# Matrix-memory gate rows: computed per tile inside the mLSTM chain, or per block of four tiles in a chain of their own

## The chip, the cores and the metric

The kernel runs on one core of a Trainium2 chip. The metric is the device time of one execution in microseconds (us), the median over several runs. The engines of the core are TensorE (PE, with the weight load PEld beside it), VectorE (DVE), ScalarE (ACT), GpSimd (POOL) and SyncE (SP), which issues the DMAs. SBUF is the on-chip memory of 128 partitions, PSUM the accumulation memory that TensorE writes. L1103 means line 1103 of the kernel.

## The reference

One layer of a hybrid encoder over 2048 prompt tokens and 8 x 16 sample tokens, width 1024, all in float32. An input projection gives queries, keys, values and gates of a matrix memory (mLSTM, 4 heads of 128) and of a sliding-window attention (8 query heads, 2 key/value heads of 64). Their outputs are joined, projected, added to the input and normalised; then come a ConvFFN (up to 2 x 2816 columns, causal convolution of width 3, gate, down to 1024) and another normalisation. What the change touches is the stabiliser of the matrix memory:

```python
b = jnp.cumsum(lf, axis=-1)                     # log forget gates, per head
inter = b + m[..., None]                        # m: running maximum carried between chunks
dmat = jnp.where(causal, b[..., :, None] - b[..., None, :] + li[..., None, :], -jnp.inf)
mt = jnp.maximum(inter, jnp.max(dmat, axis=-1))
w_inter = jnp.exp(inter - mt)
s = jnp.einsum('bhld,bhsd->bhls', qc, kc) * jnp.exp(dmat - mt[..., None])
num = w_inter[..., None] * jnp.einsum('bhld,bhde->bhle', qc, C) + jnp.einsum('bhls,bhse->bhle', s, vc)
h = num / jnp.maximum(jnp.abs(den), jnp.exp(-mt))[..., None]
m_new = jnp.maximum(b_last + m, jnp.max(g, axis=-1))    # g = b_last - b + li
```

With a = li - b this needs, for each head and token l, the running maximum M(l) of m and of all a up to l; then mt = b + M, the first weight is exp(m - M(l)) and the second exp(a(s) - M(l)) for s <= l. After a tile, m becomes b(last) + M(last).

## The kernel before

The tokens are 17 tiles of 128: 16 of the prompt, and tile 16 with the sample tokens. Matmuls run in fp32r on operands that are split into a high and a low part (three products for one); the large projections save an eighth of the products with a scheme of seven products for eight. Weights come by DMA into four raw slots and are split into high and low halves by ScalarE (L220) and VectorE (L221), into a ring of eight halves, later ten.

By the trace the stages are: the input projection (PE lines L734 and L759) until about 650 us, in four blocks of tiles (`IBLOCKS`: tiles 0 to 3 with 16, then 4 to 7, 8 to 11, 12 to 15); the output projection (L225 to L227) until about 890, in the blocks `OBLOCKS`; the up-projections of the feed-forward (L1875) from 930 to 1880; its down-projections (L2079) to the end. The work per token tile, which is little and full of waits, is woven into the dense matmuls: `t_sample` (the sample tile, 179 to 290 us), `m_chain` (the matrix memory, prompt tiles 0 to 15, 292 to 876) and `a_chain` (the attention) are generators. Each `yield cost, latency, banks` says how much PE time the step just emitted costs, how long the next step's inputs need, and how many of five PSUM banks the next step wants; `weave` emits the next step of a chain when its due time has passed by its own estimate of time. So the order of PE's instructions is fixed by these estimates when the program is built (`manual_schedule`, PE only); the order on the other engines is made by a scheduler from the data dependences and priorities. SP issues all DMAs from one queue in order.

A prompt tile in the matrix memory goes so. `m_load` issues the loads of q, k, v and the output gate. `m_rows` transposes the log gates of the tile to rows (four heads on four partitions, 128 tokens: `pgr`, L1033 and L1034), scans them for b (L1103), subtracts (L1104), scans for M with the carry `mc` as its start value (L1105), splits M in high and low for a matmul (`hilo`), makes the row -b - M (`y_row`, L1044) and the new carry. In `m_tile`, `m_rep` puts -M(l) of each head on all 128 partitions with four matmuls against a selection matrix (`pm`, L1127); `m_cols` turns the rows a and -b - M, and the carry, into columns (`pcol`, L1051 and L1052, copied to SBUF at L1055); `m_masked` adds the causal mask (L1132), and ScalarE takes exp with the column as bias: `m_inter` (L1144), `m_exps` (L1138), `m_emt` (L1060). Scores, products with v and with the state C, the state's update, the normalisation `m_norm` (its maximum is L1180) and `m_out` follow. The output stage reads the mixed rows of a block with `x_pair` (its subtraction is L926, for some of them on GpSimd).

Of the kernel before, what the change touches and what calls it, by code (L numbers as in the profile page):

```python
# [18 lines left out]
DB = 8  # L19
DS = 16  # L20
NPT = SEQ // P
NT = NPT + 1
TOK = NT * P
MH = 4
# [9 lines left out]
NBANKS = 5  # L34
HOLDS = {"pm": 6500, "pgr": 4000, "pnum": 5000, "ppo": 6500}

# [3 lines left out]
IBLOCKS = [[0, 1, 2, 3, 16], [4, 5, 6, 7], [8, 9, 10, 11], [12, 13, 14, 15]]  # L40
# [116 lines left out]
class Chains:  # L157
# [47 lines left out]
class Prog:  # L205
# [96 lines left out]
    def setup(self):  # L302
        nc, a, cp, dp = self.nc, self.a, self.cp, self.dp
# [4 lines left out]
        nc.vector.memset(self.mhalf, -0.5)  # L308
        self.zqk = [dp.tile([8, P, P * len(b)], F32, name=f"zqk{i}") for i, b in enumerate(IBLOCKS)]
        self.zws = [[dp.tile([1 if g < KEPT else 2, P, 4, HT], F32, name=f"zws{g}_{i}") for i in range(4)] for g in range(NG)]  # L310
        self.zv = [dp.tile([P, 512], F32, name=f"zv{t}") for t in range(NT)]
# [648 lines left out]
    def t_setup(self):  # L960
        nc, a, tp = self.nc, self.a, self.tp
# [17 lines left out]

        raw = self.work("kw", [36, MH])  # L980
        nc.sync.dma_start(raw, a["sel"])
        self.sel = self.one("sel", [36, MH], F32R)
        nc.vector.tensor_copy(self.sel, raw)
        self.hl = [self.one(f"hl{i}", [36, P], F32R) for i in range(2)]
        self.ay = [self.one(f"ay{i}", [36, P]) for i in range(2)]
        for i in range(2):
            nc.vector.memset(self.ay[i], 0.0)
            nc.vector.tensor_copy(self.hl[i], self.ay[i])
# [4 lines left out]
        self.mc = self.one("mc0", [MH, 1])  # L993
        nc.vector.memset(self.mc, 0.0)

# [6 lines left out]
    def gate_logs(self, b):  # L1002

        nc, tp = self.nc, self.tp
        n = len(IBLOCKS[b])
        g = tp.tile([P, 5, 8], F32, name="g1", tag="g1", bufs=2)
        nc.vector.tensor_add(g[:, :n], self.gates[b][:, :n], self.gb.rearrange("p (o m) -> p o m", o=1).to_broadcast([P, n, 8]))
        x = g[:, :n, 0:4]
# [18 lines left out]
    def row(self, nm, dt=F32):  # L1027
        return self.work("r_" + nm, [MH, P], dt, 1 if nm == "b" else 2)

    def gate_rows(self, g, i):  # L1030

        ps = self.bank([MH, 2, P], "pgr")
        self.nc.tensor.transpose(ps[:, 0], g[:, i, 0:4], self.ident)  # L1033
        self.nc.tensor.transpose(ps[:, 1], g[:, i, 4:8], self.ident)  # L1034
        return ps[:, 0], ps[:, 1]

    def hilo(self, i, src):

        nc, dst = self.nc, self.hl[i]
        nc.vector.tensor_copy(dst[0:4], src)  # L1040
        nc.vector.tensor_sub(dst[32:36], src, dst[0:4].bitcast(F32))

    def y_row(self, i, b, M):
        self.nc.vector.scalar_tensor_tensor(self.ay[i][32:36], b, -1.0, M, op0=ALU.mult, op1=ALU.subtract)  # L1044

    def m_cols(self, i, mp=None):

        nc = self.nc
        ps = self.bank([P, 40], "pcol")
        if mp is not None:  # L1050
            nc.tensor.matmul(ps[:, 0:4], mp.to_broadcast([MH, P]), self.ident[:MH, :MH], start=True, stop=True)  # L1051
        nc.tensor.transpose(ps[:, 4:40], self.ay[i], self.ident[:36, :36])  # L1052
        c0 = 4 if mp is None else 0
        col = self.work("col", [P, 40], bufs=2)
        nc.vector.tensor_copy(col[:, c0:], ps[:, c0:])  # L1055
        return col

    def m_emt(self, col):
        emt = self.work("emt", [P, MH], bufs=2)
        self.nc.scalar.activation(emt, col[:, 36:40], AF.Exp)  # L1060
        return emt

# [9 lines left out]
    def m_chain(self):  # L1072
        nc = self.nc
        while not self.chains.done["s"]:
            yield 0, 500
        pend = None
        for t in range(NPT):
            b, ti = self.place(t)
            while self.i_done <= b:
                yield 0, 500  # L1080
            if pend is None:
                pend = self.m_load(t, b, ti), *self.m_rows(t, b, ti)
                yield 300, 7000, 2
            else:
                yield 0, 1000, 2
# [4 lines left out]
            if t + 1 < NPT and self.i_done > self.place(t + 1)[0]:  # L1090
                pend = self.m_load(t + 1, *self.place(t + 1)), *self.m_rows(t + 1, *self.place(t + 1))
            yield 300, 6800, 1
            self.m_out(t, hn[0])
            self.chains.done["m"] = t
        nc.sync.dma_start(self.a["m_p"], self.mc)
        nc.sync.dma_start(self.a["cn_p"], self.C)

    def m_rows(self, t, b, ti):
        V = self.nc.vector
        lf, li = self.gate_rows(self.logs_of(b), ti)  # L1100
        i = t % 2
        bc, a_, M = self.row("b"), self.ay[i][0:4], self.row("M")
        V.tensor_tensor_scan(bc, lf, self.seg[:, 0], 0.0, op0=ALU.add, op1=ALU.add)  # L1103
        V.tensor_sub(a_, li, bc)  # L1104
        V.tensor_tensor_scan(M, self.seg[:, 0], a_, self.mc, op0=ALU.add, op1=ALU.max)  # L1105
# [16 lines left out]

    def m_rep(self, i):

        pm = self.bank([P, MH, P], "pm")
        for h in range(MH):
            self.nc.tensor.matmul(pm[:, h], self.sel[:, h:h + 1].to_broadcast([36, P]), self.hl[i], start=True, stop=True)  # L1127
        return pm

    def m_masked(self, pm, mask):  # L1130
        dt = self.work("dt", [P, MH, P])
        self.nc.vector.tensor_tensor(dt, pm, mask.rearrange("p (o m) -> p o m", o=1).to_broadcast([P, MH, P]), op=ALU.add)  # L1132
        return dt

    def m_exps(self, dt, col):

        for h in range(MH):
            self.nc.scalar.activation(dt[:, h], dt[:, h], AF.Exp, bias=col[:, 4 + h:5 + h])  # L1138

    def m_inter(self, pm, col):  # L1140

        wi = self.work("wi", [P, MH, P])
        for h in range(MH):
            self.nc.scalar.activation(wi[:, h], pm[:, h], AF.Exp, bias=col[:, h:h + 1])  # L1144
        return wi
# [61 lines left out]

    def m_tile(self, t, load, i, mp):
        nc = self.nc
        V = nc.vector  # L1210
        qk, v1, og = load
        pm = self.m_rep(i)
        col = self.m_cols(i, mp)
        dt = self.m_masked(pm, self.mcau)
        yield 600, 2800
        emt = self.m_emt(col)
        wi = self.m_inter(pm, col)
        self.m_exps(dt, col)
        yield 0, 5000, 2
# [161 lines left out]
    def t_sample(self):  # L1381
        nc, a = self.nc, self.a
        V = nc.vector
        t = NPT
# [4 lines left out]
        b, ti = self.place(t)  # L1389
        lf, li = self.gate_rows(self.logs_of(b), ti)  # L1390
        bc, M = [self.row(n) for n in ("b", "M")]
        ar = self.work("sd", [MH, P], name="ar")
        a_ = self.ay[1][0:4]
        V.tensor_tensor_scan(bc, self.seg[:, 1], lf, 0.0, op0=ALU.mult, op1=ALU.add)
# [9 lines left out]
        b3 = lambda r: r.rearrange("p (b l) -> p b l", b=DB)  # L1404
        V.tensor_sub(b3(x), b3(M), self.m0.rearrange("p (b o) -> p b o", o=1).to_broadcast([MH, DB, DS]))
        self.hilo(0, x)
        self.hilo(1, M)
        self.y_row(1, bc, M)
# [7 lines left out]
        col = self.m_cols(1)  # L1416
        dt = self.m_masked(pm, mblk)
        emt = self.m_emt(col)
        self.m_exps(dt, col)
# [751 lines left out]
```

## Time and profile before

| | |
|---|---|
| runs | 2345.95, 2350.46, 2352.51 us; median 2350.46 |
| profiled execution | 2345.55 us, span 2343.8 us |
| PE busy | 2304.7 us, 98% of the span |
| VectorE busy | 1805.6 us, 77% |
| ScalarE busy | 1298.6 us, 55% |
| GpSimd busy | 244.7 us, 10% |
| DMA | 624.98 MB, mean 267 GB/s |

The span runs from the first to the last instruction of the profiled execution; its own time is a little longer. Busy times of different engines overlap. Matmuls overlap each other too, so the time that one takes from PE is read from the distance between starts, not from its duration. In rows of a tile's instructions the three numbers behind the count are the least, the median and the greatest duration in ns, followed by the stretch of the span in which they lie.

### The profile page before, as it was taken

The page shows a single profiled execution, that of the slowest core. Times are in us where ns is not written, and L with a number is a line of the kernel's source. Part 1 is how long each engine was busy: PE and PEld are TensorE (multiplying, and loading weights), DVE is VectorE, ACT ScalarE, POOL GpSimd, SP SyncE. Part 2 cuts the span into 40 slices and gives each one's busy share as a digit, 9 for nine tenths or more (in the row PEclk, how much of TensorE's full clock was granted, in tenths as well). Part 3 has the DMA queues.
Part 4 walks back from the last instruction along what each step waited for, and adds up shares of the span by engine and source line. Part 5 has one row for each costly group of instructions (what it writes and reads, how often), then busy time and mean ns, then how long its engine had stood idle before and what let it go on. Part 6 is the DMA issues. An engine that isn't in the chain of part 4 may idle for free.

```text
span 2343.8 us, 39880 instructions
## 1 busy us (share of the span) xinstructions
PE 2304.7 (98%) x14425; PEld 2116.7 (90%) x14425; DVE 1805.6 (77%) x3150; ACT 1298.6 (55%) x2465; POOL 244.7 (10%) x298
## 2 busy tenths in 40 slices
PE   8999999999999999999999999999999999999998
PEld 8989998999987777999999999999999978888887
DVE  8676586797688888987888777768766776796897
ACT  5353466676666665555556555545544544654653
POOL 0101101101112221300001000002000100000100
PEclk9999999999999999999999999999999999999999
DMA  8888889889877667787777889878988776756753
GB/s 277 285 306 287 290 280 319 283 280 340 296 256 246 215 206 268 269 323 275 279 270 252 309 314 320 303 272 264 316 289 261 241 278 212 237 193 222 238 184 108
DMA packets 297365, 624.98 MB, mean 267 GB/s; under 512 B 47052, under 2 KB 140240, under 8 KB 297168
## 3 DMA queue, kind: packets, MB, share of 16 engines
q1 hardware_dynamic: 296304, 619.29, 77.6%
q10 hardware_dynamic: 864, 3.15, 0.4%
q8 instruction: 114, 1.87, 0.3%
q14 instruction: 83, 0.68, 0.1%
HBM read 451.78 MB, written 170.56 MB: 266 GB/s over the span
## 4 chain that ended last, share of the span: by engine, by line
PE 72%; DVE 6%; DMA 2%; issue 2%; ACT 2%; POOL 0%; SPq 0%; DVEq 0%; ACTq 0%; POOLq 0%
PE fup L1875 18%; PE dps L1875 18%; PE dps L2079 6%; PE dps L734 6%; PE fup L2079 6%; PE fht L2079 5%; PE dps L225 2%; PE dps L227 2%; PE dps L226 2%; PE ppo L1370 1%; PE psc L1321 1%; PE ppt L1364 1%; PE dps L759 1%; DVE hl L221 1%; DVE w L221 1%
## 5 line engine op out<-in xcount | busy, mean ns | idle before, releaser
L1875 PE MATMUL dps<-hh,uw 128*128 128x384 f32 (+1 forms) x1848 | 480.6, 328 | 6.8 <-ACT u L1900 1.9
L1875 PE MATMUL fup<-hh,uw 128*128 128x384 f32 (+1 forms) x1848 | 479.4, 328 | 2.8 <-ACT u L1900 2.7
L1875 PEld LDWEIGHTS dps<-hh,uw 128*128 128x128 f32 x1848 | 329.7, 188 | 11.0 <-ACT u L1900 3.0
L1923 DVE SCALAR_TENSOR_TENSOR cc<-u,cw,cc 128x768 f32<-128x768 f32 (+1 forms) x264 | 252.4, 977 | 107.7 <-ACT cc L1921 105.5
L1875 PEld LDWEIGHTS fup<-hh,uw 128*128 128x128 f32 x1848 | 329.8, 188 | 4.3 <-ACT u L1900 3.8
L1875 PE MATMUL fup<-hl,uw 128*128 128x384 f32 (+1 forms) x924 | 302.4, 327 | 0.5 <-DVE hl L221 0.5
L1875 PE MATMUL dps<-hl,uw 128*128 128x384 f32 (+1 forms) x924 | 302.0, 327 | 0.0
L734 PE MATMUL dps<-w,oh 128*128 128x256 f32 x1344 | 258.0, 286 | 4.1 <-ACT zev L800 2.7
L221 DVE TENSOR_TENSOR w<-wraw,w 128x1024 fp32r<-128x1024 f32 (+2 forms) x163 | 188.1, 1159 | 61.7 <-ACT w L220 60.6
L220 ACT CAST w<-wraw 128x1024 fp32r<-128x1024 f32 (+2 forms) x163 | 160.9, 993 | 122.6 <-PE dps L734 56.1
L734 PEld LDWEIGHTS dps<-w,oh 128*128 128x128 f32 x1344 | 213.0, 190 | 16.3 <-issue 8.9
L220 ACT CAST uw<-wraw 128x1024 fp32r<-128x1024 f32 x126 | 122.8, 977 | 184.2 <-PE dps L2079 106.4
L1921 ACT ACTIVATE cc<-u,cw 128x768 f32<-128x768 f32 (+1 forms) x132 | 129.5, 997 | 122.2 <-DVE u L1914 61.1
L221 DVE TENSOR_TENSOR uw<-wraw,uw 128x1024 fp32r<-128x1024 f32 x126 | 142.4, 1131 | 67.7 <-ACT uw L220 67.1
L734 PE MATMUL dps<-w,ol 128*128 128x256 f32 x672 | 189.1, 281 | 0.0
L734 PE MATMUL dps<-oh,w 128*128 128x256 f32 x896 | 168.8, 284 | 7.0 <-ACT oh L579 2.2
L1875 PEld LDWEIGHTS fup<-hl,uw 128*128 128x128 f32 x924 | 173.4, 188 | 1.3 <-DVE hl L221 1.3
L2079 PE MATMUL fup<-uw,fu 128*128 128x512 f32 x726 | 172.1, 393 | 1.7 <-DVE uw L221 1.7
L1875 PEld LDWEIGHTS dps<-hl,uw 128*128 128x128 f32 x924 | 173.4, 188 | 0.0
L2079 PEld LDWEIGHTS fup<-uw,fu 128*128 128x128 f32 x726 | 136.2, 188 | 33.1 <-DVE uw L221 2.2
L2079 PE MATMUL dps<-uw,fu 128*128 128x512 f32 x660 | 163.2, 393 | 0.0
L734 PEld LDWEIGHTS dps<-oh,w 128*128 128x128 f32 x896 | 140.7, 189 | 13.8 <-issue 4.1
(337 smaller groups left out, 4624.4 us busy)
## 6 DMA issues: line engine op xcount, KB each, us to landing
uw<-zw SPq DMA_DIRECT2D x176, 512.0 KB, 5.0
zw<-uw SPq DMA_DIRECT2D x88, 512.0 KB, 2.9
w<-zws SPq DMA_DIRECT2D x72, 512.0 KB, 6.6
wv<-wup SPq DMA_DIRECT2D x66, 512.0 KB, 5.8
wraw<-wi SPq DMA_DIRECT2D x64, 512.0 KB, 5.1
wraw<-zt SPq DMA_DIRECT2D x60, 512.0 KB, 4.1
wraw<-wdn SPq DMA_DIRECT2D x45, 512.0 KB, 3.9
wraw<-wo SPq DMA_DIRECT2D x40, 512.0 KB, 4.9
```

The costliest lines, as they stand in the source:

```text
L220: nc.scalar.copy(hi, src)
L221: nc.vector.tensor_sub(lo, src, hi.bitcast(F32))
L225: mm(out, ah, bh, start=start, stop=False)
L226: mm(out, ah, bl, start=False, stop=False)
L227: mm(out, al, bh, start=False, stop=stop)
L734: mm(o, l, r, start=s in (1, 7) and c == k == i == 0, stop=k == 3 and i == 2, skip_group_check=True)
L759: mm(o, x, w, start=k == i == 0, stop=k == KD - 1 and i == 2, skip_group_check=True)
L1321: nc.tensor.matmul(ps[kvh][:, j, :nk], q[rs, j0 + j], k[rs, sel], start=i == 0, stop=i == 2)
L1875: mm(ps, l[:, k], r[:, k], start=s in (1, 7) and k == 0 and i == 0, stop=k == 3 and i == 2, skip_group_check=True)
L1921: S.activation(c[:, v], u[:, v, 2:2 + n], AF.Identity, bias=w[3], scale=w[2])
L1923: V.scalar_tensor_tensor(c[:, v], u[:, v, i:i + n], w[i], c[:, v], op0=ALU.mult, op1=ALU.add)
L2079: mm(ps, l[:, k, c], r[:, k], start=s in (1, 4, 7) and u == 0 and k == 0 and i == 0, stop=u == nu - 1 and k == n - 1 and i == 2, skip_grou ...
```

## The change

A fourth generator, `g_chain`, does the gate rows for a whole block of four prompt tiles. It transposes the log gates of four tiles at once (sixteen rows: tile and head), runs both scans on sixteen rows, each tile from a start of its own, without the carry, and puts a, b and -A (A is the running maximum of the tile alone) into one tile `grow` of 80 rows. It writes -A to a DRAM buffer `zr`, and the last columns of b and -A to `zl`; then it reads `zl` back onto all partitions (`ends`). After a pause, one 80-row transpose gives the columns of the block. After another, the carry is followed from tile to tile in columns that are the same on every partition: four times a minimum and a subtraction on [128, 4] give `nmp`, the negated running maximum at the start of each tile; `mp`, and `emt` for all four tiles, follow.

For each tile `m_rows` now only reads 256 KB from `zr` with a broadcast DMA (`nm`: -A of the tile's four heads on all partitions). `m_tile` takes the minimum of `nm` and the column `nmp` on VectorE, which gives -M; `m_masked` adds the mask to it and `m_inter` reads it, from SBUF in place of PSUM. The sample tile's two rows go through DRAM (`zs`) as well, with one more pause of 4000 in its generator. The selection matrix, the tiles `hl`, one `ay`, `mc` and the PSUM tiles `pm` go. `gate_logs` stores forget and input gates apart and so has two additions in place of one. `m_chain` yields less cost, and no banks for `pm`. The program is built with a DMA scratch area of 2048 instead of its standard size, which moves many SBUF tiles to other addresses.

```diff
+        self.grow = self.one("grow", [80, P])
...
-        self.live = [[p.t_sample(), 0.0, 0], [p.m_chain(), 0.0, 0], [p.a_chain(), 0.0, 0]]
+        self.live = [[c, 0.0, 0] for c in (p.t_sample(), p.m_chain(), p.a_chain(), p.g_chain())]
...
+    def g_chain(self):
+        nc, V = self.nc, self.nc.vector
+        last = None
+        while not hasattr(self, "glog"):
+            yield 0, 500
+        for b in range(len(IBLOCKS)):
+            while self.i_done <= b:
+                yield 0, 500
+            n = 4 * MH
+            lf, li = self.gate_rows(self.logs_of(b), 0, 4)
+            R = self.grow
+            bc, A = self.row("b"), self.row("M")
+            V.tensor_tensor_scan(bc, lf, self.zero4, 0.0, op0=ALU.add, op1=ALU.add)
+            V.tensor_sub(R[0:n], li, bc)
+            V.tensor_tensor_scan(A, self.zero4, R[0:n], -3e38, op0=ALU.add, op1=ALU.max)
+            V.tensor_scalar_mul(R[64:64 + n], A, -1.0)
+            V.tensor_copy(R[32:32 + n], bc)
+            col1 = lambda z, c: z[:, c * n:(c + 1) * n].rearrange("o (r m) -> (o r) m", m=1)
+            nc.sync.dma_start(self.zr[b].rearrange("o (r m) -> (o r) m", m=P), R[64:64 + n])
+            nc.sync.dma_start(col1(self.zl[b], 0), R[32:32 + n, P - 1:P])
+            nc.sync.dma_start(col1(self.zl[b], 1), R[64:64 + n, P - 1:P])
+            ends = self.work("ends", [P, 2, 4, MH])
+            nc.sync.dma_start(ends.rearrange("p a t h -> p (a t h)"), self.zl[b].to_broadcast([P, 2 * n]))
+            yield 220, 4000, 1
+            ps = self.bank([P, 80], "pcol")
+            nc.tensor.transpose(ps, R, self.ident[:80, :80])
+            col = self.work("col", [P, 80], bufs=2)
+            V.tensor_copy(col, ps)
...
+            yield 110, 4000
+            for i in range(4):
+                V.tensor_tensor(nmp[:, i + 1], nmp[:, i], ends[:, 1, i], op=ALU.min)
+                V.tensor_sub(nmp[:, i + 1], nmp[:, i + 1], ends[:, 0, i])
+            last = nmp
...
     def m_chain(self):
...
-            while self.i_done <= b:
+            while b not in self.mg:
                 yield 0, 500
             if pend is None:
-                pend = self.m_load(t, b, ti), *self.m_rows(t, b, ti)
-                yield 300, 7000, 2
+                pend = self.m_load(t, b, ti), self.m_rows(b, ti)
+                yield 0, 7000
...
-    def m_rows(self, t, b, ti):
-        V = self.nc.vector
-        lf, li = self.gate_rows(self.logs_of(b), ti)
-        i = t % 2
-        bc, a_, M = self.row("b"), self.ay[i][0:4], self.row("M")
-        V.tensor_tensor_scan(bc, lf, self.seg[:, 0], 0.0, op0=ALU.add, op1=ALU.add)
-        V.tensor_sub(a_, li, bc)
-        V.tensor_tensor_scan(M, self.seg[:, 0], a_, self.mc, op0=ALU.add, op1=ALU.max)
-        self.hilo(i, M)
-        self.y_row(i, bc, M)
-        mp, self.mc = self.mc, self.work("mc", [MH, 1], bufs=3)
-        V.tensor_add(self.mc, bc[:, P - 1:P], M[:, P - 1:P])
-        return i, mp
+    def m_rows(self, b, ti):
+        nm = self.work("nm", [P, MH, P])
+        self.nc.sync.dma_start(nm.rearrange("p h m -> p (h m)"), self.zr[b][:, ti * MH * P:(ti + 1) * MH * P].to_broadcast([P, MH * P]))
+        a, nmp, mp, emt = self.mg[b]
+        return nm, a[:, ti], nmp[:, ti], mp[:, ti], emt[:, ti]
...
-    def m_rep(self, i):
-        pm = self.bank([P, MH, P], "pm")
-        for h in range(MH):
-            self.nc.tensor.matmul(pm[:, h], self.sel[:, h:h + 1].to_broadcast([36, P]), self.hl[i], start=True, stop=True)
-        return pm
...
-    def m_tile(self, t, load, i, mp):
+    def m_tile(self, t, load, rows):
...
-        pm = self.m_rep(i)
-        col = self.m_cols(i, mp)
-        dt = self.m_masked(pm, self.mcau)
-        yield 600, 2800
-        emt = self.m_emt(col)
-        wi = self.m_inter(pm, col)
-        self.m_exps(dt, col)
+        nm, a, nmp, mp, emt = rows
+        V.tensor_tensor(nm, nm, nmp.rearrange("p (h o) -> p h o", o=1).to_broadcast([P, MH, P]), op=ALU.min)
+        dt = self.m_masked(nm, self.mcau)
+        yield 0, 2200
+        wi = self.m_inter(nm, mp)
+        self.m_exps(dt, a)
...
     def t_sample(self):
...
+        nc.sync.dma_start(rows[0], x)
+        nc.sync.dma_start(rows[1], nM)
...
-        wi = self.work("wi", [P, MH, P])
-        nc.scalar.activation(wi, self.m_rep(0), AF.Exp)
-        pm = self.m_rep(1)
+        wi, nm = self.work("wi", [P, MH, P]), self.work("nm", [P, MH, P])
+        for i, z in enumerate((wi, nm)):
+            nc.sync.dma_start(z.rearrange("p h m -> p (h m)"), self.zs[:, i * MH * P:(i + 1) * MH * P].to_broadcast([P, MH * P]))
+        yield 0, 4000
...
-    nc = bacc.Bacc("TRN2", target_bir_lowering=False, num_devices=1)
+    nc = bacc.Bacc("TRN2", target_bir_lowering=False, num_devices=1, dynamic_dma_scratch_size=2048)
```

More of the change, by code (lines that the diff above doesn't have):

```diff
@@ L34 @@
 NBANKS = 5
-HOLDS = {"pm": 6500, "pgr": 4000, "pnum": 5000, "ppo": 6500}
+HOLDS = {"pgr": 4000, "pnum": 5000, "ppo": 6500}
 WB = 4
@@ L978, in t_setup @@
         nc.vector.tensor_scalar_mul(self.gm, self.gm, 0.5)
[L980 to L988, printed above, removed]
+        self.ay = self.one("ay", [36, P])
+        nc.vector.memset(self.ay, 0.0)
+        self.grow = self.one("grow", [80, P])
+        nc.vector.memset(self.grow, 0.0)
+        self.zero4 = self.one("zero4", [4 * MH, P])
+        nc.vector.memset(self.zero4, 0.0)
+        self.mg = {}
         self.kh, self.kl = [self.one(n, [P, RING, P], F32R) for n in ("kringh", "kringl")]
@@ L1063, in place, with y_row, m_cols @@
+    def y_row(self, b, M):
+        self.nc.vector.scalar_tensor_tensor(self.ay[32:36], b, -1.0, M, op0=ALU.mult, op1=ALU.subtract)
+    def m_cols(self):
+        nc = self.nc
+        ps = self.bank([P, 36], "pcol")
+        nc.tensor.transpose(ps, self.ay, self.ident[:36, :36])
+        col = self.work("cols", [P, 36])
+        nc.vector.tensor_copy(col, ps)
+        return col
     def place(self, t, blocks=IBLOCKS):
```

104 lines of the change are left out of this document (53 added, 51 removed).

## The prediction

> **What bounds the kernel now.** I read the busy times and slices first, then the chain that ended last, then stage windows, then the tiles that the change touches and the waits around them.
>
> ```profile
> span 2343.8 us, 39880 instructions
> PE 2304.7 (98%) x14425; PEld 2116.7 (90%) x14425; DVE 1805.6 (77%) x3150; ACT 1298.6 (55%) x2465; POOL 244.7 (10%) x298
> DMA  8888889889877667787777889878988776756753
> PE 72%; DVE 6%; DMA 2%; issue 2%; ACT 2%; POOL 0%; SPq 0%; DVEq 0%; ACTq 0%; POOLq 0%
> ```
>
> TensorE (PE) is busy for 98% of the span and carries 72% of the chain. By stage (columns: window, length, then the busy time of each engine, granted clock, DMA share, GB/s):
>
> ```profile
> core 0: us, PE busy (x) PEld busy (x) DVE busy (x) ACT busy (x) POOL busy (x), PEclk, DMA share, GB/s
> 485.00:633.00 148.00, 147.98 (x1244) 137.12 (x1244) 109.26 (x344) 99.86 (x264) 18.42 (x18) 1.00 0.92 312
> 760.00:890.00 130.00, 128.55 (x726) 101.14 (x725) 109.00 (x292) 80.77 (x211) 31.71 (x20) 1.00 0.63 210
> ```
>
> Where the mLSTM tiles run (485 to 890, tile 0 from 292) PE stands for about 1% of the time, so any matmul taken out there is time taken off the end, unless PE comes to wait for something new. The feed-forward stages from 930 on are not touched.
>
> **What leaves PE.** Per prompt tile the change removes two gate transposes (L1033, L1034), four matmuls that copy the running maximum to all partitions (L1127) and the column matmuls (L1051, L1052); the sample tile loses eight of L1127. Matmuls overlap, so I price them by distances between starts. PE's timeline around the last tile and around the sample tile (start, duration, engine, line, operation, shape):
>
> ```profile
> 841.72 0.40 PE L227 MATMUL dps<-w,ol 128*128 128x512 f32 x1
> 841.96 0.27 PE L1033 MATMUL pgr<-ident,g 128*4 128x128 f32 x1
> 842.07 0.27 PE L1034 MATMUL pgr<-ident,g 128*4 128x128 f32 x1
> 842.09 0.48 PE L225 MATMUL dps<-w,oh 128*128 128x512 f32 x1
> 842.41 0.39 PE L226 MATMUL dps<-w,oh 128*128 128x512 f32 x1
> ...
> 852.77 0.39 PE L226 MATMUL dps<-w,oh 128*128 128x512 f32 x1
> 853.00 0.40 PE L227 MATMUL dps<-w,ol 128*128 128x512 f32 x1
> 853.32 0.66 PE L1127 MATMUL pm<-hl,sel 36*128 36x128 f32 x4
> 853.91 0.38 PE L1051 MATMUL pcol<-ident,mc 4*128 4x4 f32 x2
> 854.22 0.25 PE L1052 MATMUL pcol<-ident,ay 36*128 36x36 f32 x1
> 854.40 0.65 PE L1370 MATMUL ppo<-pth,kva 128*64 128x512 f32 x2
> ...
> 190.54 1.11 PE L1127 MATMUL pm<-hl,sel 36*128 36x128 f32 x8
> 191.49 0.22 PE L1052 MATMUL pcol<-ident,ay 36*128 36x36 f32 x1
> ```
>
> One dense matmul starts 0.23 after the one before it (852.77 to 853.00). From 841.72 to 842.41 is 0.69, of which L227 and L225 are 0.46: the transpose pair costs 0.23. From 853.00 to 854.40 is 1.40, less L227's 0.23: the copying and column group costs 1.17. So 16 x 1.40 = 22.4, and the sample's eight L1127 add 0.95 (190.54 to 191.49): **23.35 us leave PE**. The new chain does, once per block of four tiles, a transpose pair of 16 instead of 4 rows (0.23, the form's 128 columns being the same) and one 80-row transpose in place of 36 (estimate 0.3, up from 0.25): 4 x 0.53 = 2.1. **Net -21.2 us of PE work.**
>
> **The new wait on PE.** PE runs its orders strictly in sequence, so at the 80-row transpose it stands until VectorE has finished the five gate operations that follow the transpose pair. In the order written for the changed kernel 42, 42, 30 and 15 dense matmuls (the last two with a dozen chain matmuls) lie between; at 0.119 for an input-projection matmul (147.98 us over 1244, above) and 0.23 for one of the output projection that is 4.4 to 5.4 us, mean 4.9. How long VectorE takes is bounded by the same lag now, first and last tile:
>
> ```profile
> 292.92 0.42 PE L1034 MATMUL pgr<-ident,g 128*4 128x128 f32 x1
> 295.28 0.28 DVE L1044 SCALAR_TENSOR_TENSOR ay<-r_b,r_M 4x128 f32<-4x128 f32 x1
> 851.63 0.28 DVE L1044 SCALAR_TENSOR_TENSOR ay<-r_b,r_M 4x128 f32<-4x128 f32 x1
> ```
>
> It is 2.6 us (to 295.56) for tile 0 and 9.8 (842.07 to 851.91) for tile 15, where VectorE had other work first. The work itself is short:
>
> ```profile
> L1103 DVE TENSOR_TENSOR_SCAN r_b<-pgr,k_seg x16: 380/404/411, 293.8 to 847.3; 4x128 f32<-4x128 f32 x16
> L1104 DVE TENSOR_TENSOR ay<-pgr,r_b x16: 269/272/279, 294.2 to 848.9; 4x128 f32<-4x128 f32 x16
> L1105 DVE TENSOR_TENSOR_SCAN r_M<-k_seg,mc,ay x16: 462/466/473, 294.5 to 850.8; 4x128 f32<-4x128 f32 x16
> L1132 DVE TENSOR_TENSOR dt<-pm,k_mcau x16: 635/682/692, 304.9 to 858.5; 128x512 f32<-128x512 f32 x16
> L221 DVE TENSOR_TENSOR w<-wraw,w 128x1024 fp32r<-128x1024 f32 (+2 forms) x163 | 188.1, 1159 | 61.7 <-ACT w L220 60.6
> ```
>
> Sixteen rows in place of four keep the 128 columns, so 0.404 + 0.272 + 0.466 and two small row operations of some 0.2 make 1.54 us. In blocks 2 and 3 they stand nearly alone in VectorE's order and end within the lead: 0.2 us each. In blocks 0 and 1 they stand behind sample or state work, one addition and one weight split (1.159): I take 7 us against 4.9, so 2.2 each. Sum **+4.8**; bounds 0 (lag 2.6) and 4 x 4.9 = 19.6 (lag 9.8).
>
> **The trip through DRAM.** The block's last column goes to DRAM and comes back on all partitions (`ends`); eight small VectorE operations wait for it, and behind them in VectorE's order stand the splits of the weights that PE wants. SP, which issues every DMA from one queue, waits in front of these writes for VectorE, and before the load for the write's landing; the weight loads queue behind. The rows nearest to the price:
>
> ```profile
> k_sinkx<-sinkx SPq DMA_DIRECT2D x1, 0.5 KB, 4.4
> ...
> SPq L461 <- DVE w L221: 36.3, 23, 5.2
> ...
> PE dps L734 <- DMA w<-zws: 0.2, 1, 0.2
> ...
> L1676 SPq DMA_DIRECT2D lnp<-ln_b x2: 422/1012/1602, 938.2 to 992.0; - x2
> ...
> DMA to landing us min/median/max: 3.8/4.7/5.5
> ```
>
> The first row ends with the time to landing; the two rows of waits give the sum, the count and the longest. The last two are of the tile `lnp`, the kernel's broadcast loads of 256 KB. A 0.5 KB transfer landed in 4.4 us and a broadcast in 4.7: 9.1, and up to 14.3 with SP's longest wait for a split, 5.2. Ahead of the first use VectorE has other work: two splits, a copy and an addition in block 0 (3.2 us), 6.5 to 8 in the others. So VectorE stands for (9.1 - 3.2) + 3 x (9.1 - 7.5) = 10.7 us in all. PE feels it only once the splits made ahead are used up: one split unit feeds 24 matmuls of 0.119, or 2.9 us, and the ring holds four units, 11 us when full. PE waited 0.2 us on a weight load in the whole stretch, so I take **+2** (block 0's excess over one or two units); bounds 0 and the rival C below.
>
> **Edits that cost PE nothing.** VectorE loses per tile the scans, the subtraction, the hi/lo casts and a column copy (some 2.2 us) and gains a minimum of 128x512 with both inputs in SBUF (0.58, half of L221, to 0.68, L1132) and a fourth of 3.7 us per block: 1.6. It stays about 10 us lighter; it is 77% busy. ScalarE's four exponentials per tile read SBUF instead of PSUM: under 0.05 each. The 18 broadcast loads of 256 KB are 4.7 MB against 624.98, and each is issued with the loads of q, k, v some 30 us ahead of use, so its 4.7 us are covered, also where DMA is at 0.92; without that cover each would cost up to 4.7. The sample's two loads and its longer pause (+4) lie behind the sample chain, which PE fills with input projection. The m chain's fewer pauses bring its tiles forward by a microsecond or two, and the attention chain is late next. The smaller DMA scratch moves SBUF tiles; weight loads over ten slots now do not differ by place:
>
> ```profile
> L1875 PEld LDWEIGHTS dps<-hl,uw x924: 187/188/192, 946.3 to 1874.7; 128*128 128x128 f32 x185
> ```
>
> **Sum:** -21.2 + 4.8 + 2 = -14.4. The profiled execution took 2345.55 us, 1.75 more than its span and 4.9 less than the median 2350.46 of the runs. So 2345.55 becomes 2331.1, and the median **2336**. Within the forecast the waits may come to half or one and a half times mine and the transposes to 0.5 either way: -9 to -19, 2331 to 2341. The three runs span 6.6 us, so 0.3% (7 us) is what can be told from no change.
>
> **Rivals.** *A, the waits are hidden.* VectorE's five operations end inside the lead in each block, as tile 0's 2.6 us would, and the splits cover the trip: -21.2, 2329. Against it: tile 15's 9.8 us. Chance 0.18.
>
> *B, no change.* Each block's transpose waits the full 4.9 us: -21.2 + 19.6, 2349. For it: VectorE 74 to 84% busy in the windows; against it: the position in its order. The change then has shortened PE's work but not its time. Chance 0.16.
>
> *C, slower: the trip through DRAM holds VectorE.* At 14.3 us per trip and 3.2 of cover VectorE is held 11.1 in each block; if PE then has only one unit (2.9) in hand it stands 8.2, four times 33. -21.2 + 4.8 + 33 = +17, 2367. It decides from 5.3 us of PE standing per block. For it: SP waited for a split 23 times (36.3 us in 230 to 660), so a write can be late behind it; against it: PE's 0.2 us of weight waits. Chance 0.13.
>
> *D, slower: VectorE and GpSimd block each other.* The minimum and the mask addition now have both inputs in SBUF (the mask's was PSUM). The trace shows what such a pair can do:
>
> ```profile
> L1180 DVE TENSOR_TENSOR mr<-mr,emt x17: 145/150/1855, 226.7 to 875.8; 128x4 f32<-128x4 f32 x17
> ...
> 843.15 1.85 DVE L1180 TENSOR_TENSOR mr<-mr,emt 128x4 f32<-128x4 f32 x1
> 842.60 2.39 POOL L926 TENSOR_TENSOR ol<-xraw,oh 128x1024 fp32r<-128x1024 f32 x1 [0.75 <-ACT mr L1176]
> ```
>
> A VectorE operation of 0.15 took 1.85, ending at 845.00 as GpSimd's (842.60 + 2.39 = 844.99) did. That is 1.7 us lost; 32 operations make 54 of VectorE at most, and GpSimd is busy 24% of 760 to 890, where six tiles are: 2 x 1.7 x 6 = 20 on the path at worst. -14.4 + 20 = +6, 2356; it decides from 14 us. Against it: VectorE is no bound elsewhere. Chance 0.07. [...]
>
> **How the numbers follow.** Forecast 0.46, A 0.18, B 0.16, C 0.13, D 0.07. Time 2336. Faster by over 0.3%: forecast and A, 0.64; within: B, 0.16; slower: C and D, 0.20. The range takes in A, B and D, with 3 us (half of the runs' distance) beyond: 2326 to 2359, leaving out C and the tails.
>
> **What would show it.** Right: PE's busy time down by about 21; 80-row transposes preceded by PE idle of 0 to 3 us released by VectorE, four times; VectorE idle before the first minimum of the `ends` line, longest in block 0, with PE's waits on L221 hardly changed; span between 485 and 890 shorter by some 14; from 930 on the same distances. Wrong: idle on PE before dense matmuls released by L221 right after each block's load (C); the new minimum taking over 1 us beside GpSimd (D); PE idle of 5 us at each 80-row transpose (B); broadcast loads landing after VectorE asks for them; or distances changed in the feed-forward stages, which nothing above explains.

## The result

The changed kernel takes 2355.14 us (median; 2352.79 to 2360.84), the kernel before 2349.4 in the same comparison: ratio 1.0027, 95% interval 1.0019 to 1.0036, so about 6 us slower. Forecast were 2336 and a gain of 14. The time lies within the stated range (2326 to 2359), but the sign is wrong.

The profiled execution of the changed kernel took 2354.49 us. From its page, the busy times and the chain that ended last:

```profile
span 2352.7 us, 39587 instructions
PE 2294.3 (98%) x14285; PEld 2108.8 (90%) x14285; DVE 1792.5 (76%) x3108; ACT 1297.6 (55%) x2453; POOL 244.7 (10%) x298
...
PE 76%; DVE 10%; DMA 6%; ACT 3%; issue 3%; POOL 1%; SPq 0%; DVEq 0%; ACTq 0%; POOLq 0%
```

PE's busy time is down by 10.4 us while the span is up by 8.9 (more than the 6 of the medians, because the profiled execution of the kernel before, 2345.55, was faster than all 14 of its runs here), and DMA has gone from 2% to 6% of the chain. Busy time alone misleads here, because matmuls take longer at half clock: in the changed kernel those of L737 start 0.21 us apart where the granted clock is 0.50 (531.40 to 533.96) and 0.12 apart where it is 1.00 (529.82 to 530.87). The stretch from 12 us to the first up-projection matmul of the feed-forward that writes the tile `dps` (called the first up-projection below; the very first ones, into `fup`, start some 12 to 15 us sooner), of the kernel before, of the changed kernel, and of the run `all_three` told below (columns as in the prediction's windows):

```profile
12.00:946.30 934.30, 918.52 (x6833) 824.90 (x6832) 722.73 (x1716) 552.69 (x1273) 138.51 (x99) 0.99 0.82 277
```

```profile
12.00:954.50 942.50, 908.10 (x6691) 816.24 (x6691) 709.85 (x1676) 550.72 (x1261) 138.80 (x99) 0.99 0.84 279
```

```profile
12.00:933.10 921.10, 902.83 (x6698) 813.16 (x6698) 705.92 (x1676) 551.40 (x1261) 137.34 (x99) 0.99 0.84 286
```

PE was not busy for 15.8 us of it before (934.30 - 918.52) and for 34.4 after. I split the time to the first up-projection matmul in three: PE's idle gaps over 0.15 us from 12 us on, the time lost at reduced clock (one minus the granted clock, summed over windows of 2 us), and the rest, which is PE working at full clock together with the first 12 us:

| profiled execution of | first up-projection at | idle | lost at half clock | rest |
|---|---|---|---|---|
| before | 946.3 | 15.3 | 5.1 | 925.9 |
| after | 954.5 | 34.1 | 13.7 | 906.7 |
| difference | +8.2 | +18.8 | +8.6 | -19.2 |

So the matmuls did leave PE, 19.2 us against a forecast net of 21.2, and 27.4 us came back: 18.8 of idle time and 8.6 of half clock. (Idle time that falls into a stretch at half clock stands in both columns: 0.9 us after, none before.) From there on little changes: evictions of the up-projections come 8.1 us later than before at 958 us and at 1263, the down-projections 9.1 later at 1946 and at 2259.

Who PE waited for between 170 and 950 us in the changed kernel (total, count, longest):

```profile
PE pcol L1064 <- DVE grow L1054: 5.8, 2, 3.6
PE dps L737 <- ACT dps L831: 3.3, 2, 2.9
PE dps L762 <- DVE zev L809: 3.1, 1, 3.1
PE dps L737 <- DMA w<-zws: 3.1, 2, 1.7
PE ppt L1385 <- ACT pth L1386: 2.5, 2, 1.4
PE dps L737 <- ACT zev L792: 2.4, 1, 2.4
```

Only the first row is the wait that I forecast. The others are copies out of PSUM and weights that come late, and the waits of VectorE (170 to 900 us) show a cause that I had set at nothing:

```profile
DVE nm L1235 <- DMA nm<-zr: 16.5, 8, 5.4
DVE nmp L1074 <- DMA ends<-zl: 10.6, 4, 4.9
```

The second row is the block ends, 10.6 us where I had worked out 10.7. The first is the per-tile broadcast load, which I had called covered. One of its eight waits on VectorE's and SP's timelines:

```profile
452.92 0.28 DVE L221 TENSOR_TENSOR kringl<-pk,kringh 128x128 fp32r<-128x128 f32 x1
458.58 0.69 DVE L1235 TENSOR_TENSOR nm<-nm,nmp 128x512 f32<-128x512 f32 x1 [5.38 <-DMA nm<-zr]
459.31 0.69 DVE L1154 TENSOR_TENSOR dt<-nm,k_mcau 128x512 f32<-128x512 f32 x1
459.92 1.22 DVE L221 TENSOR_TENSOR w<-wraw,w 128x1024 fp32r<-128x1024 f32 x1
```

```profile
446.93 0.50 SPq L1144 DMA_DIRECT2D qk<-zqk x1
450.78 0.83 SPq L785 DMA_DIRECT2D zog<-zev x2
451.66 1.05 SPq L1149 DMA_DIRECT2D og<-zog x1
452.75 0.67 SPq L1137 DMA_DIRECT2D nm<-zr x1
```

The load is issued at 452.75, VectorE reaches the minimum at 453.20 and stands 5.38 us, with a weight split (459.92) behind it. The buffer of `nm` was not what kept the load: the tile before had read it for the last time by 416. In SP's queue the load stands behind the others of its tile and behind stores of the projection (L785), 5.8 us after the load of `qk`; at 602 the distance is 13. Only one of the eight loads that VectorE waited for (498.53) was issued just as its buffer came free.

The half clock, in windows of the changed kernel around PE's wait of 2.88 us for L831 (ScalarE's copy of one PSUM accumulator to another), which ends at 529.59:

```profile
526.00:530.00 4.00, 1.12 (x10) 0.93 (x9) 3.48 (x15) 1.17 (x4) 0.10 (x1) 1.00 0.83 327
530.00:534.00 4.00, 4.00 (x25) 4.00 (x25) 4.00 (x18) 4.00 (x13) 0.00 (x0) 0.62 0.75 218
534.00:538.00 4.00, 4.00 (x35) 4.00 (x35) 4.00 (x10) 3.21 (x8) 0.00 (x0) 0.95 1.04 343
```

After the gap PE runs about 3.4 us at half clock (by the granted clock 0.38 x 4 + 0.05 x 4 = 1.7 lost). This wait of 2.9 so cost 4.6.

### The profile page after: what moved, and what is told of

Its sections match the earlier page's. It is cut to its first block, busy times and chain, and to the rows that moved or that the text cites. A ratio compares the mean times of both kernels' runs of the same rounds, so it can differ in the third digit from the quotient of the medians.

```text
span 2352.7 us, 39587 instructions
## 1 busy us (share of the span) xinstructions
PE 2294.3 (98%) x14285; PEld 2108.8 (90%) x14285; DVE 1792.5 (76%) x3108; ACT 1297.6 (55%) x2453; POOL 244.7 (10%) x298
## 4 chain that ended last, share of the span: by engine, by line
PE 76%; DVE 10%; DMA 6%; ACT 3%; issue 3%; POOL 1%; SPq 0%; DVEq 0%; ACTq 0%; POOLq 0%
PE dps L1902 18%; PE fup L1902 18%; PE dps L737 11%; PE dps L2106 6%; PE fup L2106 6%; PE fht L2106 6%; DVE w L221 2%; PE dps L762 1%; PE ppo L1391 1%; PE dps L225 1%; PE dps L227 1%; PE dps L226 1%; DMA wraw<-wi 1%; PE psc L1342 1%; ACT w L220 1%
## 5 line engine op out<-in xcount | busy, mean ns | idle before, releaser
L737 PE MATMUL dps<-w,oh 128*128 128x256 f32 x1344 | 258.2, 287 | 9.2 <-DMA w<-zws 3.1
L737 PEld LDWEIGHTS dps<-w,oh 128*128 128x128 f32 x1344 | 213.2, 191 | 22.1 <-issue 10.0
L737 PE MATMUL dps<-w,ol 128*128 128x256 f32 x672 | 189.5, 282 | 0.0
L737 PE MATMUL dps<-oh,w 128*128 128x256 f32 x896 | 173.0, 288 | 6.7 <-ACT dps L831 2.9
L737 PEld LDWEIGHTS dps<-oh,w 128*128 128x128 f32 x896 | 144.8, 195 | 12.7 <-issue 4.1
```

What stands on the lines that cost most here:

```text
L737: mm(o, l, r, start=s in (1, 7) and c == k == i == 0, stop=k == 3 and i == 2, skip_group_check=True)
```

## The experiments

Theory: VectorE stands for loads that have not landed, PE then for VectorE, and the half clock adds to it. Rivals: the waits at the 80-row transpose are the loss; the trip of the block ends is; or VectorE's new order is, and not its standing. Ratios are to the kernel before, with 95% intervals; the changed kernel has 1.0027.

**A longer first pause.**

```diff
-            yield 220, 4000, 1
+            yield 220, 9000, 1
```

> The changed kernel with the first pause of the gate chain 9000 instead of 4000, so that more dense matmuls stand between the transposes of a block and its 80-row transpose. Theory (the waits and the half clock behind them eat the gain): PE's waits of 2.2 and 3.6 us at the 80-row transposes go, and with the second the two half-clock stretches at 346 to 354 (3.4 us lost): about 9 us less than the changed kernel's 2355, 2346. Rival (VectorE is late in any case and PE waits for something else instead): 0 to 2 us less, 2353 to 2355.

Measured: 2353.7, ratio 1.0019 (1.0005 to 1.0033). PE no longer waits at the 80-row transposes (5.8 us before), but its idle time fell only from 34.1 to 28.6, with new waits (2.08 at 343.8, 1.64 at 384.3). The rival holds: the wait that I forecast is there, and taking it away alone gives back little, since VectorE, ScalarE and weight loads are late next.

**Only a little longer a pause**, 5000, as a measure of how much a rebuilt order moves the time.

> The changed kernel with the gate chain's first pause 5000 instead of 4000: hardly an edit, meant to show how far the time moves when the order of the other engines shifts a little. If single edits are told apart by their own mechanism: within 3 us of the changed kernel, 2352 to 2358. Rival (each rebuilding shuffles waits, as the undone sample part hints with 13 us more instead of 4 less): off by 5 us or more either way.

Measured: 2351.01, ratio 1.0011 (0.9999 to 1.0023), 1 us outside the first expectation. The wait at the transposes is 1.8 us instead of 5.8, so it isn't as idle an edit as I had meant. By the ratios it took 4 us off, more than the pause of 9000, which took 2. Differences of up to some 4 us between two kernels here are not to be explained.

**The minimum written to the tile of the weights `wi`**, so that `nm` is free at once; the next tile's load is issued right behind.

```diff
-        V.tensor_tensor(nm, nm, nmp..., op=ALU.min)
-        dt = self.m_masked(nm, self.mcau)
+        wi = self.work("wi", [P, MH, P])
+        V.tensor_tensor(wi, nm, nmp..., op=ALU.min)
+        if t + 1 < NPT and self.place(t + 1)[0] in self.mg:
+            n = self.place(t + 1)
+            self.nms[n] = self.nm_load(*n)
+        dt = self.m_masked(wi, self.mcau)
```

> The changed kernel with the minimum written to the tile of the inter-chunk weights instead of in place, so that the broadcast tile is free at once and the next tile's load is issued right behind the minimum, one tile earlier. Theory (VectorE stands 16.5 us for these loads and hands it on to PE): VectorE's idle time before the minimum falls from 16.5 to under 4 us; PE's waits for evictions at 479, 529 and 610 (8.4 us) and the two half-clock stretches with them (3.4) go: 8 to 12 us less, 2343 to 2347. Rival (those waits of PE come from VectorE's other order, not from its standing): VectorE's idle time falls all the same and the time stays within 2 us of 2355.

Measured: 2342.15, ratio 0.9977 (0.9967 to 0.9986): 12 us off the changed kernel, and faster than the kernel before. No wait for `nm<-zr` is left on VectorE; this is the only large row of a load:

```profile
DVE nmp L1074 <- DMA ends<-zl: 13.2, 4, 5.3
```

Half of what I expected of PE did not come, though. In the profiled execution (2347.7, the slowest of the twelve) PE's wait at 610 is gone and the one at 479 is down to 1.46, but that for L831 is still there (3.08 at 526), with a stretch at half clock behind it (granted clock 0.80, 0.50 and 0.85 in the windows of 2 us from 526 on); PE's idle time is 31.2, the half clock's loss 8.5. The minimum also stands later in VectorE's order now, in eleven of the sixteen tiles by one to eleven splits, so the run left open whether the standing or the place had mattered. The next one tells them apart.

**One load of the rows for all tiles**, tile 0's, with the minimum in place as in the changed kernel.

```diff
-        nm = self.work("nm", [P, MH, P])
-        self.nc.sync.dma_start(nm..., self.zr[b][:, ti * MH * P:(ti + 1) * MH * P]...)
+        if (b, ti) == (0, 0):
+            self.nm0 = self.one("nm0", [P, MH, P])
+            self.nc.sync.dma_start(self.nm0..., self.zr[b][:, :MH * P]...)
+        nm = self.nm0
```

> The changed kernel with the rows of tile 0 loaded once and used by every tile, so that no tile waits for its own broadcast load (the minimum stays in place and may stand earlier in VectorE's order, not later; the output is not the layer's). Tells apart why the minimum in the weights' tile gained 12 us. If it was VectorE's standing for the loads: VectorE's wait before the minimum under 3 us in all and 2341 to 2347. If it was the later place of the minimum in VectorE's order: 2352 to 2356.

Measured: 2344.31, ratio 0.9976 (0.9967 to 0.9986), the same as with the early load, with the minimum no later in the order (as many splits stand ahead of it in seven tiles, fewer in nine). What the two runs have in common is that VectorE no longer stands for these loads. By the ratios the early load gains 12 us alone, 12 with the longer pause and 16 with the ends by matmul (both below), so the gain does not hang on one order: the standing costs 11 us or more. The 4 MB of traffic that this run also leaves out add nothing that can be seen, since the early load, which keeps them, gains as much.

How the standing reaches PE I can follow at one place, 610 us in the changed kernel:

```profile
608.22 0.69 DVE L1235 TENSOR_TENSOR nm<-nm,nmp 128x512 f32<-128x512 f32 x1 [3.79 <-DMA nm<-zr]
608.99 0.69 ACT L1166 ACTIVATE wi<-nm,mp 128x128 f32<-128x128 f32 x2 [5.87 <-DVE mq L1205]
609.59 0.57 ACT L792 ACTIVATE zev<-dps 128x512 f32<-128x512 f32 x1
610.22 0.39 PE L737 MATMUL dps<-w,oh 128*128 128x256 f32 x1 [2.41 <-ACT zev L792]
```

VectorE stands for the load, ScalarE's exponentials for VectorE, the eviction L792 behind them in ScalarE's order, and PE for that eviction. In both runs without the standing this wait is gone. The rest of the gain is spread: the first up-projection comes 9.5 us sooner than in the changed kernel in both, but with 31.2 of idle time and 8.5 at half clock in one and 25.3 and 14.6 in the other.

**No trip of the block ends**; a tile of zeros stands in place of the loaded one, so this kernel leaves the carry out.

```diff
-            nc.sync.dma_start(col1(self.zl[b], 0), R[32:32 + n, P - 1:P])
-            nc.sync.dma_start(col1(self.zl[b], 1), R[64:64 + n, P - 1:P])
-            ends = self.work("ends", [P, 2, 4, MH])
-            nc.sync.dma_start(ends..., self.zl[b].to_broadcast([P, 2 * n]))
+            ends = self.ends0
```

> The changed kernel without the trip of the block ends through DRAM: a tile of zeros, set once, stands in place of the loaded one, and the two small writes and the load of each block are left out, so the carried maximum is not the layer's. Prices what VectorE's 10.6 us before the end columns cost. Theory of the prediction (2 us of it reach PE): 2353. Rival C (VectorE is held and PE with it, 8 us a block): 2335 or less. Rival (all of it is covered): 2355.

Measured: 2349.9, ratio 1.0005 (0.9993 to 1.0018): 5 us off the changed kernel, where I had put 2 and the rival 20 or more. That is hardly more than the pause of 5000 moved.

**The block ends by a matmul**, with the right values: beside the 80-row transpose the last column, repeated, is multiplied with columns of the identity.

```diff
+            nc.tensor.matmul(ps[:, 80:], R[:, P - 1:P].to_broadcast([80, P]), self.ident[:80, 32:80], start=True, stop=True)
```

> The changed kernel with the block ends brought to all partitions by a matmul instead of through DRAM, all else as changed: the trip's price again, with the right values. If leaving the trip out was worth 5 us by itself: 2350 + 1 of PE for the matmuls, 2349 to 2353; the waits for the per-tile rows stay (16 us of VectorE). Rival (the 5 us came from the other data or from the order): 2354 to 2357.

Measured: 2352.26, ratio 1.0009 (0.9999 to 1.0020): 4 us off by the ratios, in line with 5 less the matmuls, and as near to what cannot be told.

**Combinations.** Early load and long pause:

> The minimum written to the weights' tile (early load of the next tile's rows) and the first pause of 9000 together. If the waits at the 80-row transpose cost by themselves: 2342 less 5.4 of PE idle and one half-clock stretch (1.7), 2335 to 2337. Rival (as with the longer pause alone, PE's wait turns into waits for evictions and weights): 2340 to 2343.

Measured: 2340.61, ratio 0.9969 (0.9958 to 0.9980). The rival again: no more than 2 us for the pause.

Early load and ends by matmul:

> The minimum written to the weights' tile, and the block ends brought to all partitions by one matmul beside the 80-row transpose (the last column of the 80 rows, repeated, against 48 columns of the identity) instead of the trip through DRAM. Leaving the trip out took 5 us off the changed kernel. If the stands of VectorE add up: 2342 - 5 + 4 x 0.3 of PE = 2338 (2336 to 2340). Rival (with the early load VectorE has slack enough to cover the trip): 2341 to 2344.

Measured: 2334.43, ratio 0.9942 (0.9929 to 0.9955), lower than expected: the two edits gave 12 and 4 singly, and 20 together, so behind the early load the trip is worth 8.

All three:

> Early load, longer first pause, and the block ends by matmul. Theory (the waits of VectorE and PE that the change brought, and the half clock they trigger, are the whole of what was lost, so without them PE's saved 19 us come through): 2331 to 2337. Rival (waits of this order turn up elsewhere with any order, at 10 us or so): 2338 to 2343.

Measured: 2334.43 (2332.52 to 2336.32), ratio 0.9942 (0.9929 to 0.9956). This version beats both kernels. Its waits of PE, 170 to 950 us:

```profile
PE dps L737 <- DMA w<-zws: 3.3, 2, 1.8
PE fup L1905 <- ACT fup L1918: 2.2, 1, 2.2
PE dps L762 <- DVE zev L809: 1.8, 1, 1.8
PE ppo L1394 <- ACT pth L1389: 1.4, 2, 0.7
```

In the terms of the table above it has 18.0 us idle, 8.9 at half clock and 906.2 of rest: the idle time is back to within 3 us of the kernel before and PE's saved work comes through. Against the kernel with the early load and the pause, the ends by matmul gained 6. The profiled execution's first up-projection stands at 933.1, 13.2 earlier than before.

**The sample tile's rows by matmuls, as before the change**, first in the changed kernel, then in the version with all three edits (the selection matrix, `hl` and `m_rep` return for that tile alone).

> The changed kernel with the sample tile's two rows spread by matmuls again, as before the change, its DRAM rows and extra pause gone; the prompt tiles stay as changed. Theory (the sample chain runs some 7 us later for its trip, and SP then holds the weight loads at 240 to 246 behind stores that wait for the rotary additions): PE's 3.1 us of waits for weights at 253 and the half clock behind them (1.7) go, the half clock at 302 may go (1.7), 0.95 of matmuls come back: 3 to 6 us less, 2349 to 2352. Rival (that wait is chance of the order): within 1 us of 2355, with a wait of the same size elsewhere between 180 and 300.

> Early load, longer pause and ends by matmul, and the sample tile's rows spread by matmuls as before the change. If the sample's trip through DRAM costs what the waits for weights at 250 show (3.3 us of idle, 1.7 to 5 of half clock) less 0.95 of matmuls: 2329 to 2332. Rival (undoing it upsets the order as it did in the changed kernel, 13 us up): 2336 or more.

Measured: 2367.92, ratio 1.0085 (1.0070 to 1.0099), and 2344.09, ratio 0.9976 (0.9964 to 0.9989): slower by 13 and 10 us, against the expected gain. In the first PE's idle time rose to 44.1 us and the half clock's loss to 17.1, with waits at 420, 489, 600, 710 and 962, hundreds of microseconds behind the sample tile; its largest row:

```profile
PE dps L737 <- ACT dps L831: 7.7, 4, 3.5
```

Moving the sample's rows to DRAM is thus a gain in both settings, though the matmuls that it saves are worth 0.95. Why is not settled: the orders of all engines differ from there on, and no run isolates which difference it is. An edit of this size can thus move the time by 10 us and more for a reason that these runs do not show, which is why the price of the per-tile loads rests on several pairs and not on one.

**The smaller DMA scratch alone**, in the kernel before.

> The kernel before with the smaller DMA scratch area alone, which moves its SBUF tiles. My prediction set it at nothing: 2349, within 3 us of the kernel before. Rival (the moved tiles slow weight loads or DMA writes): 2352 or more.

Measured: 2347.83, ratio 1.0000 (0.9991 to 1.0010). The moved tiles cost nothing. In the terms of the table its profiled execution has 17.8 idle, 4.2 at half clock and 926.8 of rest, so entries of that table can move by 2.5 us where nothing but addresses differs.

## Why the prediction was wrong

**The step that failed** is in the edits that were to cost PE nothing: "The 18 broadcast loads of 256 KB ... each is issued with the loads of q, k, v some 30 us ahead of use, so its 4.7 us are covered". The 30 us belong to q, k and v, whose first use is the scores; the first use of `nm` is the minimum, at the head of the tile's work. In the written order the load stands two pauses, 6.8 and 1.0, ahead of it; in the trace VectorE came to the minimum 0.45 us after the issue in the case shown. The time to landing was 4.6 to 7.5 us, median 5.8, near the 4.7 that I had. Had I applied the sentence that stood behind it, "without that cover each would cost up to 4.7", to the order of VectorE (eight waits of 2 us on the mean), it would have been the largest term after PE's own. The price of this standing, 11 to 12 us against nothing in the sum, is shown by two runs that remove the standing in different ways.

**The term that was missing**: no step priced what an idle PE costs beyond its idle time. The half clock took 8.6 us more than before. It was to be seen in the trace of before, which has three such stretches of 1.7 us lost each (at 162, 264 and 292; the first behind a window of 3.41 us in which PE was idle for 1.91, the other two behind windows without idle time), and I left it out. Even with all three edits 2.7 us of idle time and 3.8 of half clock more than before remain, 6.5 that no run here takes out.

**The trip of the block ends.** The length of VectorE's standing was right (10.7 against 10.6), its price too low: 2 us forecast, 4 to 5 measured alone, which is near the noise of the orders, and 6 and 8 with the early load. The argument "PE feels it only once the splits made ahead are used up" overlooked a way that does not pass the splits. Block 2 of the changed kernel shows it:

```profile
525.57 0.16 DVE L1074 TENSOR_TENSOR nmp<-nmp,ends 128x4 f32<-128x4 f32 x1 [4.88 <-DMA ends<-zl]
528.84 0.21 ACT L1083 ACTIVATE emt<-emt 128x16 f32<-128x16 f32 x1 [5.50 <-DVE emt L1082]
528.96 0.58 ACT L831 COPY dps<-dps 128x512 f32<-128x512 f32 x1
529.59 0.39 PE L737 MATMUL dps<-oh,w 128*128 128x256 f32 x1 [2.88 <-ACT dps L831]
```

ScalarE's exponential `emt` stands 5.50 us for the rows that VectorE makes from the ends; the copy L831 stands behind it, and PE waits for the copy. This wait stays in both runs without the standing for the per-tile loads (3.08 at 526, 3.33 at 529), and is gone in both that only take out the trip. Rival C (33 us) did not come, rightly held to be unlikely; the sign on its side did, by another load.

**The wait at the 80-row transposes** came as said: 2.15 and 3.62 us in blocks 0 and 1 against 2.2 each, nothing worth a row in blocks 2 and 3. As a term of a sum it was wrong to add it: without it the time fell by 2 us only, within what these runs can tell.

```profile
347.32 0.39 PE L1064 MATMUL pcol<-ident,grow 80*128 80x80 f32 x1 [3.62 <-DVE grow L1054]
```

**Two slips in the sums.** 7 against 4.9 gives 2.1 for a block and 4.6 in all, not 2.2 and 4.8. And the 5.3 us per block from which C decides the sign leave out the transposes; with their 4.8 it is 4.1. Neither changes the forecast by more than 0.2.

**PE's work** was right in kind, 19.2 for 21.2. **VectorE** got lighter by 13 us, as forecast 10, and that helped nothing, since what counted was where it stood, not how long it worked. ScalarE's exponentials of `wi` took 0.393 us each with their input in SBUF and 0.373 with it in PSUM (medians), within the 0.05 that I had set.

**Rival D** was small. Of 16 minima one took 1.37 instead of 0.69 (at 406.71), beside a GpSimd product that ended 0.54 before it; of 17 mask additions the sample's took 1.79 instead of 0.68 (at 201.13), also beside one: 1.8 us of VectorE in all, of the 54 that were the bound. That its time, 2356, is the one measured is chance.

```profile
L1235 DVE TENSOR_TENSOR nm<-nm,nmp x16: 673/690/1366, 209.9 to 825.7; 128x512 f32<-128x512 f32 x16
```

**What came true by chance.** The forecast time, 2336, is what the kernel takes (2334.4) once the two loads no longer hold VectorE. But the sum counts 6.8 us for waits at the transposes and the ends that this version does not have, and the version has the 6.5 of other idle time and half clock instead. That the measured time lies in the range is luck as well: the range was drawn wide for B and D.

## What to carry to other kernels

When a value that PE spread over the partitions is sent through DRAM instead, the question is where the first instruction that reads it stands in its engine's order: find that instruction, not the first use of the loads issued beside it, and what stands ahead of the load in the queue that issues it. VectorE, busy for 76% of the span and not the bound, still passed its stands in front of loads on to what was queued behind them, and to the queue of ScalarE, which waited for its results; at 529 and 610 us that reached PE through ScalarE's copies out of PSUM, for which nothing is made ahead (VectorE stood 4.88 and 3.79 us, ScalarE 5.50 and 5.87, PE 2.88 and 2.41). The gap on PE cost more than its length where the clock dropped behind it (2.88 at 529 and 1.7 more), and two stands removed together gave more (20 us) than one by one (12 and 4).

## What the runs showed of the hardware

Between 12 us and the first up-projection, in the traces of before and after, each stretch at half clock (granted clock 0.50) lasted 3.41 us and cost 1.7 by the granted clock, or twice that where two follow each other (346.68 to 353.51 in the changed kernel, 3.4 lost around a gap of 3.62). In the changed kernel's trace all of them start whole multiples of 3.41 apart: those at 254.52, 302.31, 346.68, 479.80 and 531.00 are 14, 13, 39 and 15 times 3.413 us from one to the next. I cut that trace into windows of 3.41 us along this grid. Those around the gaps of 2.15 us at 187, 3.14 at 480, 2.88 at 530 and 2.41 at 610 (window, length, PE busy; PEclk is third from the end):

```profile
182.84:186.25 3.41, 2.30 (x21) 2.10 (x19) 3.18 (x10) 2.10 (x3) 0.00 (x0) 1.00 0.65 214
186.25:189.67 3.42, 2.37 (x20) 2.40 (x21) 2.25 (x5) 0.00 (x0) 0.00 (x0) 1.00 0.49 13
476.38:479.79 3.41, 0.27 (x3) 0.06 (x2) 3.41 (x6) 3.41 (x13) 0.00 (x0) 1.00 0.61 188
479.79:483.20 3.41, 3.41 (x16) 3.41 (x17) 3.24 (x5) 3.14 (x6) 0.00 (x0) 0.50 0.92 276
527.58:531.00 3.42, 1.41 (x12) 1.41 (x13) 3.28 (x13) 2.17 (x6) 0.00 (x0) 1.00 0.49 187
531.00:534.41 3.41, 3.41 (x19) 3.41 (x18) 3.41 (x19) 3.41 (x12) 0.00 (x0) 0.50 0.99 294
606.09:609.50 3.41, 1.72 (x16) 1.52 (x14) 1.28 (x3) 0.51 (x2) 0.00 (x0) 1.00 0.91 351
609.50:612.91 3.41, 2.13 (x16) 1.89 (x16) 0.71 (x4) 2.53 (x7) 1.01 (x1) 1.00 0.69 264
```

PE was idle for 3.14 and 2.01 us of the second and third pair's first window, and the next one ran at half clock. The first and the last gap lie across the border of two windows (1.11 and 1.05 idle, 1.69 and 1.28), and no stretch followed them. In the two traces, up to the first up-projection, every window at full clock with 1.91 us of idle time or more (one before, five after) was followed by one at half clock, and of those with 1.7 or less only three, which had no idle time at all (two before, one after). The wait at the first 80-row transpose, 2.15 us without a stretch behind it in the changed kernel, had one in the run with the early load: there PE was idle for 1.56 us of 186 to 188 and 0.60 of 188 to 190, and the granted clock was 0.82, 0.50 and 0.83 in the windows of 2 us from 188 on, a stretch from about 189.3. Whether a given wait also cost 1.7 was so in part chance.

Less idle time than that also went with a drop elsewhere: in the run with the ends by matmul PE was idle for 0.73 us of 848 to 850 and 0.55 of 850 to 852, and the granted clock was 0.52 from 852 to 854. In the kernel before the clock dropped at 264 us without any gap, while matmuls of 64 columns (`ppo`, L1546 and L1547, two in 0.26 us) of the sample attention ran:

```profile
262.00:264.00 2.00, 2.00 (x18) 1.46 (x17) 0.04 (x1) 0.37 (x1) 0.00 (x0) 1.00 0.82 302
264.00:266.00 2.00, 2.00 (x11) 1.63 (x12) 0.42 (x1) 0.00 (x0) 0.00 (x0) 0.60 0.58 150
266.00:268.00 2.00, 2.00 (x12) 2.00 (x11) 0.00 (x0) 0.00 (x0) 0.00 (x0) 0.55 0.06 16
```
